# Stick-breaking attention on one core: merging the last two key blocks, holding GpSimd for scans, and re-spacing the filler matmuls

## The chip, the cores and the metric

The kernel runs on one core of one Trainium2 chip. The metric is device time in microseconds for one execution. Besides the plain time of several runs there is one profiled execution: every instruction of every engine with its start and its duration. The engines are TensorE (PE, with its weight loads as PEld), VectorE (DVE), ScalarE (ACT), GpSimd (POOL) and SyncE (SP, which only issues DMAs here).

## The reference, cut to what matters

One decoder block: RMSNorm, then a short-convolution branch and an attention branch in parallel on the same normalised input, both gated and merged, then a gated MLP. 1040 positions (16 meta tokens and 1024 real ones), width 1024, 16 heads of 64. The change lies in the attention:

```python
z = einsum(qb, kb) * scale                # one block of 128 queries, all earlier keys
log_beta = log_sigmoid(z)
log_fail = where(causal, log_beta - z, 0)
survive = cumsum(log_fail, reverse) - log_fail
a = where(causal, exp(log_beta + survive), 0)
o = einsum(a, vb)
```

So the weight of key s for query t is sigmoid(z_ts) times the product of (1 - sigmoid(z_tj)) over the keys j between s and t: a running product from the diagonal backwards.

## The kernel before, in words

**Stages.** The program has a first stage of projections (Strassen products on TensorE, up to about 670 us of the span), the attention stage (about 670 to 1028 us), a stage with the branch projections (to about 1160 us), and then the output projection and the MLP (to the end at 1966 us). Numbers are fp32 split into a high and a low fp32r part (`split`, `low`), so one product is two or three matmuls.

**The planner.** The first three stages are not written out in order. `Plan.add` collects tasks with an engine, an estimated cost, a key (a due time on the planner's own clock), dependencies, and slots that the task takes and frees (PSUM banks and buffers). `Plan.run` plays them through: whenever an engine is free it starts the ready task with the lowest key whose slots are free, and calls its `emit`, which writes the instructions. At the end `in_program_order` pins this order on each engine, so an engine that waits for one instruction also holds all behind it. The planner has a slot called `port`, one in number: GpSimd tasks and those VectorE tasks that are marked `port` (the scans at L900 among them), or that may run on either engine (`ANY`), exclude each other in planned time. On the chip nothing enforced that.

**Attention.** There are 8 pairs of heads (`p`, `h`), and the 1026 kept queries go in 9 blocks of 114 (`b`), three at a time (`g` = 0, 1, 2), which makes 48 units. In a unit each of the three query blocks gets its scores `z` on TensorE (L883, L884), ScalarE turns them into `fl` = sigmoid(-z) (L889), and VectorE runs a scan over the keys from the back (L900), 128 + 114 b elements long. Then `fl` is turned key block by key block: `turn` transposes into a PSUM bank `tp` (L919), ScalarE casts it to `ah` (L924), VectorE subtracts for the low part `al` (`low`, recorded as L353), and `weigh` multiplies both with the values into `av` (L934, L935). A unit has 3 g + 3 key blocks; to all but the last two belong three query blocks (342 columns), to the last but one two (228 columns), to the last one one (114). So the last two blocks are two steps with a bank, a cast and a subtraction each.

**A unit's end.** ScalarE copies half of `av` into the single buffer `half` (`out1`, L957), the rest into `ot` (`out2`, L960), and GpSimd adds `half` to `ot` (`out3`, L964), which frees `half`. After a pair's six units GpSimd adds the term `ends` to all 1026 columns in one operation (`last_add`, L977), and the pair is stored to DRAM.

**Fillers.** TensorE's other work in the stage are plain products (L253 to L255): two gate items and six convolution items, each 24 steps of three matmuls of 342 columns. Their weights come through ScalarE (`whi`, L367) and GpSimd (`wlo`, L275). All 24 steps of an item have keys within about 11 us of planned time; gates start at key 0 and 20, convolution items at 50 plus about 52 for each. The convolution items need the rows `y`, which take the place of the gates' input and therefore come after the last gate; `split_rows` loads, casts (L1009) and subtracts each row of 1026 columns in one operation on VectorE or GpSimd.

Of the kernel before, what the change touches and what calls it, by code (L numbers as in the profile page):

```python
# [35 lines left out]
class Plan:  # L36
    LAG = {"PE": 0.22, "ACT": 0.18, "DVE": 0.13, "POOL": 0.13, "SP": 2.5, None: 0.0}

    def __init__(self, slots, since=None):
        self.slots = dict(slots, port=1)  # L40
        self.free = dict(since.free) if since else dict.fromkeys(Plan.LAG, 0.0)
        self.tasks = []

    def add(self, engine, cost, emit, after=(), key=0.0, takes=(), frees=(),
            port=False):
        t = SimpleNamespace(engine=engine, cost=cost, emit=emit, key=key, takes=tuple(takes),
                            frees=frees, port=port or engine in ("POOL", "ANY"), users=[], left=0, number=len(self.tasks))
# [10 lines left out]
    def run(self):  # L58
        events, count, done, free = [], 0, 0, self.free
        now = free["PE"]  # L60
        ready = {e: [] for e in Plan.LAG}

        def enter(t):
            for e in ("DVE", "POOL") if t.engine == "ANY" else (t.engine,):
                insort(ready[e], (t.key, t.number, t))

        for t in self.tasks:
            if t.left == 0:
                enter(t)
        for at in free.values():  # L70
            if at > now:
                heappush(events, (at, count, True, None))
                count += 1
        while done < len(self.tasks):
            moved = True
            while moved:
                moved = False
                for e in Plan.LAG:
                    if e is not None and free[e] > now + 1e-9:
                        continue  # L80
                    for i, (_, _, t) in enumerate(ready[e]):
                        if (not t.port or self.slots["port"]) and all(
                                self.slots[k] >= t.takes.count(k) for k in t.takes):
                            break
                    else:
                        continue
                    del ready[e][i]
# [59 lines left out]
def block_kernel(ctx, tc, x, meta_tokens, g_pre_mix, w_in, channels, w_proj_conv,  # L147
# [198 lines left out]
    pin_from = len(nc.cur_bb.bb.instructions)  # L346
    plan = Plan({"raw": 2, "whi": 0, "wlo": 0, "ap": 4, "wk": 5, "st": 8, "xw": 2, "gt": 1})
# [28 lines left out]
    def plain(o, chunks, key, evac, finish, psum, first_chunk=0, given=None, w=w_in, src=src_x,  # L376
              ready=(), eng="ANY", by="ACT", lead=16.0, space=("wk",), after=()):
# [5 lines left out]
        for ci in range(first_chunk, 3):  # L383
# [7 lines left out]
            for kb in range(KB):  # L391
                at = key + (8 * (ci - first_chunk) + kb) * 3 * pe_cost(CH)
# [444 lines left out]
    FL = [2] * 6 + [1] * 3  # L837
    plan = Plan({"raw": 1, "whi": 1, "wlo": 1, "mm": 2, "z": 2, "tp": 3, "av": 1, "qk": 2, "vv": 1,
# [11 lines left out]
    DELAY = 0.6 * half_pair  # L850
    out_tiles = {}
    av_last = last_turn = None
    for p in range(NPAIR):
        ot_parts = []
        v_ld = None
        v_users = []
        for h in range(2):
# [9 lines left out]
            for g in range(3):  # L867
# [40 lines left out]
                for kb in range(nkb):  # L908
                    k0, n = KEYS[kb]
                    bs = [b for b in range(3 * g, 3 * g + 3) if P + QB * b > k0]  # L910
                    off = QB * (bs[0] - 3 * g)
                    kst = {}
                    t_k = t_av + share[g] * half_pair * kb / nkb

                    def turn(k0=k0, n=n, bs=bs, g=g, kst=kst, fls=fls):
                        tp = kst["tp"] = ps_tp.tile([P, 512], F32, name="tp", tag="tp")
                        for b in bs:
                            j = b - 3 * g
                            nc.tensor.transpose(tp[:n, QB * j:QB * (j + 1)], fls[b]["fl"][:, k0:k0 + n],  # L919
                                                ident[:QB, :QB])  # L920

                    def high(n=n, off=off, kst=kst):
                        kst["ah"] = work.tile([P, CH], F32R, name="ah", tag="ah", bufs=4)
                        nc.scalar.copy(kst["ah"][:n, off:], kst["tp"][:n, off:CH])  # L924

                    def lower(n=n, off=off, kst=kst):
# [3 lines left out]
                    def weigh(kb=kb, n=n, off=off, h=h, nkb=nkb, kst=kst, ust=ust, p=p):  # L930
                        if kb == 0:
                            ust["av"] = ps_av.tile([P, 512], F32, name="av", tag="av")[:, :CH]
                        av, w = ust["av"], v_tiles[p][:n, kb, h, :]
                        nc.tensor.matmul(av[:, off:], w, kst["ah"][:n, off:], start=(kb == 0), stop=False)  # L934
                        nc.tensor.matmul(av[:, off:], w, kst["al"][:n, off:], start=False,  # L935
                                         stop=(kb == nkb - 1))

                    m = CH - off
                    tt = plan.add("PE", 0.098 * len(bs) + 0.02, turn, (last_turn, *(scans[b] for b in bs)), t_k, ("tp",))
# [3 lines left out]
                    hh = plan.add("ACT", act_cost(m), high, (tt,), t_k, ("ah",))  # L943
                    ll = plan.add("DVE", dve_cost(m), lower, (hh,), t_k, ("al",), ("tp",))
                    last_av = plan.add("PE", 2 * pe_cost(m) + 0.08, weigh, (hh, ll, v_ld, last_av), t_k + 1,
                                       ("av",) if kb == 0 else (), ("ah", "al"))
# [24 lines left out]
                ot_parts.append(plan.add("POOL", pool_cost(CH), out3, (o1, o2), t_o, (), ("half",)))  # L971
            plan.join(z_users, ("qk",))
        plan.join(v_users, ("vv",))

        def last_add(e="POOL", p=p):
            ov = out_tiles[p][:, :NQ].rearrange("p (b n) -> p b n", n=QB)
            engine_of(e).tensor_tensor(ov, ov, ends[:, p].unsqueeze(2).to_broadcast([P, 9, QB]), op=ALU.add)  # L977
# [3 lines left out]
        plan.add("SP" if q is nc.sync else "ACT", cost, lambda p=p, q=q: q.dma_start(  # L981
            o_d[p * P:(p + 1) * P, :], out_tiles[p][:, :NQ]), (fin,), t_o + 1, (), ("ot",))
# [6 lines left out]

    nxt[0]["los"] = nxt[1]["load"] = None  # L990
    mid_last = []
    for i, (which, ob) in enumerate(mid_gates):
        evac, finish = gate_out(which, ob, work_tile, ("wk",))

        def ended(evacs, key, finish=finish):
# [3 lines left out]
        plain(48 + 8 * which + ob, CH_Q, 20.0 * i, evac, ended, bank_mm, 0, nxt[i],  # L999
              eng="POOL", lead=34.0)  # L1000

    def split_rows(kb, parts, src_d, key, after, begin=None, takes=()):
# [8 lines left out]
        def lower(e):  # L1011
            hi, lo = parts()
# [4 lines left out]
        return plan.add("ANY", any_cost(NQ), lower, (t,), key)  # L1017
# [14 lines left out]
    def conv_item(ob, key, tile_of, psum, ready, given=None):  # L1032
# [10 lines left out]
        def finish(evacs, key):  # L1043
# [5 lines left out]
              34.0, (), (ld,))  # L1049

    y_open = plan.add(None, 0.0, open_y, tuple(mid_last))
    y_ready = [split_rows(kb, lambda kb=kb: feats["y", kb], y_d, 24.0 + 2.5 * kb, (y_open,))
               for kb in range(KB)]
# [724 lines left out]
```

## Time and profile before

| | |
|---|---|
| median of 3 runs | 1968.5 us (1965.8 to 1968.56) |
| the profiled execution's own time | 1968.02 us |
| its span, first to last instruction | 1966.1 us |
| mean granted TensorE clock | 0.993 |
| TensorE matmuls | 12876 |
| scans (L900) | 144 |
| transposes (L919) | 720 |
| casts `ah` and subtractions `al` | 288 each |

A row of the grouped view reads: line, engine, operation, written tile, read tiles, shape, count, then busy us and mean ns of one, then idle time of the engine just before these instructions and what ended it. A row of the windows view reads: the stretch in us, its length, then the busy us of each engine with the number of instructions that start in it, the granted clock of TensorE as a share of full speed, the share of the DMA engines, and GB/s. A row of the timeline reads: start us, duration us, engine, line, operation, tiles, shape, count, and in brackets idle time before it. Several equal neighbours are merged into one row with a count.

### The profile page before, as it was taken

What the parts mean: (1) busy time and instruction counts of PE and PEld (TensorE: products, weight loads), DVE (VectorE), ACT (ScalarE), POOL (GpSimd) and SP (SyncE); (2) the same over time, 40 slices, a digit from 0 to 9 for tenths busy, and PEclk for the clock granted to TensorE, in tenths of its full rate; (3) what the DMA queues carried; (4) which work ended last, traced back from release to release, by engine and by line L of the source; (5) the groups of instructions that cost most, each with busy time, mean ns of one, the idle gap of its engine ahead of it and who ended that gap; (6) DMA issues with size and microseconds to landing.
All of it is one profiled execution on the core that took longest, in us unless ns stands there. A gap on an engine that the chain in (4) does not pass through costs nothing. (4 is left out here: it accounts for less than half of the span.)

```text
span 1966.1 us, 32363 instructions
## 1 busy us (share of the span) xinstructions
PE 1909.8 (97%) x12876; PEld 1793.0 (91%) x12876; DVE 1194.9 (61%) x1820; ACT 858.5 (44%) x1786; POOL 600.2 (31%) x404
## 2 busy tenths in 40 slices
PE   6999999999999999999989999899999999999997
PEld 6999999999999988999979999779889988888886
DVE  6936666665644289999973356864444454355547
ACT  5533333344444376767772224444433444321122
POOL 1110000000000023332353311256565656553453
PEclk9999999999999999999999999999999999999999
DMA  3522121455443786564427753222222121342224
GB/s 141 166 76 87 65 71 59 132 153 156 151 135 95 177 238 185 148 174 132 122 82 220 219 158 111 76 86 76 75 75 97 65 86 65 129 165 93 86 86 139
DMA packets 73842, 238.56 MB, mean 121 GB/s; under 512 B 15400, under 2 KB 17224, under 8 KB 72668
## 3 DMA queue, kind: packets, MB, share of 16 engines
q1 hardware_dynamic: 70224, 225.48, 37.3%
q10 hardware_dynamic: 3468, 11.03, 1.7%
q8 instruction: 101, 1.65, 0.4%
q14 instruction: 49, 0.40, 0.1%
HBM read 166.02 MB, written 70.46 MB: 120 GB/s over the span
## 5 line engine op out<-in xcount | busy, mean ns | idle before, releaser
L709 PE MATMUL st<-tT,s_op 128*128 128x260 f32 x864 | 245.3, 284 | 0.0
L712 PE MATMUL st<-tT,s_op 128*128 128x260 f32 x864 | 244.4, 283 | 0.0
L711 PE MATMUL st<-tT,s_op 128*128 128x260 f32 x864 | 244.3, 283 | 0.0
L184 POOL TENSOR_TENSOR a_op<-raw,a_op 128x512 fp32r<-128x512 f32 (+1 forms) x136 | 194.6, 1444 | 98.8 <-ACT a_op L183 92.2
L900 DVE TENSOR_TENSOR_SCAN fl<-fl,upper 114x128 f32<-114x128 f32 (+5 forms) x144 | 203.6, 1431 | 21.2 <-ACT fl L889 20.9
L709 PE MATMUL st<-xnT,s_op 128*128 128x260 f32 x648 | 183.1, 283 | 0.0
L712 PE MATMUL st<-xnT,s_op 128*128 128x260 f32 x648 | 182.9, 282 | 0.0
L711 PE MATMUL st<-xnT,s_op 128*128 128x260 f32 x648 | 182.3, 281 | 0.0
L1394 PE MATMUL st<-opT,a_op 128*128 128x258 f32 (+2 forms) x528 | 171.0, 324 | 3.6 <-ACT snap L1409 1.9
L353 DVE TENSOR_TENSOR s_op<-raw,s_op 128x512 fp32r<-128x512 f32 x157 | 109.9, 701 | 105.0 <-ACT s_op L665 104.5
L1396 PE MATMUL st<-opT,a_op 128*128 128x258 f32 (+2 forms) x528 | 169.3, 321 | 1.8 <-DVE opT L184 1.5
L665 ACT CAST s_op<-raw 128x512 fp32r<-128x512 f32 x162 | 100.2, 621 | 161.4 <-PE st L712 153.0
L1398 PE MATMUL st<-opT,a_op 128*128 128x258 f32 (+2 forms) x528 | 168.9, 320 | 0.0
L712 PEld LDWEIGHTS st<-tT,s_op 128*128 128x128 f32 x864 | 163.1, 189 | 0.0
L711 PEld LDWEIGHTS st<-tT,s_op 128*128 128x128 f32 x864 | 162.7, 188 | 0.0
L709 PEld LDWEIGHTS st<-tT,s_op 128*128 128x128 f32 x864 | 162.5, 188 | 0.0
L1693 DVE TENSOR_TENSOR acc<-acc,st 128x512 f32<-128x512 f32 x144 | 98.4, 686 | 90.3 <-PE st L1688 90.3
L183 ACT CAST a_op<-raw 128x512 fp32r<-128x512 f32 (+1 forms) x136 | 85.2, 634 | 155.2 <-DMA raw<-in_w_up_gate_dram 50.6
L187 DVE TENSOR_TENSOR raw<-raw 128x512 f32<-128x512 f32 x86 | 81.9, 952 | 109.7 <-POOL a_op L184 107.5
L924 ACT CAST ah<-tp 114x342 fp32r<-114x342 f32 (+3 forms) x288 | 104.5, 404 | 60.9 <-PE tp L919 58.8
L353 DVE TENSOR_TENSOR al<-tp,ah 114x342 fp32r<-114x342 f32 (+3 forms) x288 | 114.8, 439 | 24.8 <-ACT ah L924 24.1
L1396 PE MATMUL st<-opB,a_op 128*128 128x512 f32 (+2 forms) x396 | 127.6, 322 | 1.9 <-DVE opB L184 1.7
(241 smaller groups left out, 5497.5 us busy)
## 6 DMA issues: line engine op xcount, KB each, us to landing
raw<-in_w_in_dram SPq DMA_DIRECT2D x64, 512.0 KB
raw<-in_w_up_gate_dram SPq DMA_DIRECT2D x44, 512.0 KB
act_d<-owork SPq DMA_DIRECT2D x22, 512.0 KB
araw<-act_d SPq DMA_DIRECT2D x22, 512.0 KB
raw<-in_w_down_dram SPq DMA_DIRECT2D x22, 512.0 KB
qh<-qh_d SPq DMA_DIRECT2D x32, 256.5 KB
ql<-ql_d SPq DMA_DIRECT2D x32, 256.5 KB
vv_d<-vt SPq DMA_DIRECT2D x16, 512.0 KB
```

What stands on the lines that cost most here:

```text
L184: (lo_engine or nc.vector).tensor_tensor(lo, src, hi.bitcast(F32), op=ALU.subtract)
L353: eng.tensor_tensor(out, src, hi.bitcast(F32), op=ALU.subtract)
L665: nc.scalar.copy(ops[name][:, 0], src())
L709: nc.tensor.matmul(ps, wt[:, 0, c], xh, start=start and kb == 0, stop=False, skip_group_check=True)
L711: nc.tensor.matmul(ps, wt[:, 0, c], xl, start=False, stop=False, skip_group_check=True)
L712: nc.tensor.matmul(ps, wt[:, 1, c], xh, start=False, stop=kb == 3, skip_group_check=True)
L900: nc.vector.tensor_tensor_scan(fl[:, ::-1], fl[:, ::-1], upper[:, NT - nk:][:, ::-1], 1.0, op0=ALU.mult, op1=ALU.max)
L924: nc.scalar.copy(kst["ah"][:n, off:], kst["tp"][:n, off:CH])
L1394: nc.tensor.matmul(ps, wt[:, 0, k], xh, start=start and kb == 0, stop=False, skip_group_check=True)
L1396: nc.tensor.matmul(ps, wt[:, 0, k], xl, start=False, stop=False, skip_group_check=True)
L1398: nc.tensor.matmul(ps, wt[:, 1, k], xh, start=False, stop=stop and kb == 3, skip_group_check=True)
L1693: nc.vector.tensor_tensor(a, a, ps, op=ALU.add)
```

## The change

Six edits:

1. **Two key blocks in one step.** The last two key blocks of a unit share a bank: the last block's 114 columns go to the front of `tp`, the last but one's 228 behind them. One cast and one subtraction of 342 columns replace 228 and 114. The transposes and the matmuls stay the same in number and columns.
2. **Held GpSimd operations.** Where the planner starts a GpSimd task later than the task and the engine were ready (for the port, or for a buffer), the first instruction of that task now waits on a semaphore for the last port operation that was planned on VectorE. This holds for all three planned stages.
3. **Transposes in groups.** When TensorE's last task was a `turn`, the planner prefers another ready `turn` whose key is at most 2.0 behind the lowest; the planned cost of leaving a run of transposes is now 0.08 us once, instead of 0.02 per `turn` and 0.08 per `weigh`. The delay of turns behind scores goes from 0.6 to 0.7 of a head's planned time.
4. **Smaller pieces.** `last_add` runs per group of three query blocks (342 columns, three per pair) instead of once per pair, and the subtraction of `split_rows` runs in three pieces of 342 columns, each on VectorE or GpSimd.
5. **Fillers' keys spread.** A gate's steps are 2.5 times as far apart (gates at keys 0 and 30), a convolution item's 3.5 times (items at 70 plus 44 each).
6. **Buffers.** The tiles `fl0` to `fl5`, `ot` and `wk` are allocated first, so that they lie next to `upper`. Numbers and sizes of buffers stay.

The core of the diff:

```diff
 class Plan.run:
-                    for i, (_, _, t) in enumerate(ready[e]):
-                        if (not t.port or self.slots["port"]) and all(
-                                self.slots[k] >= t.takes.count(k) for k in t.takes):
+                    best = None
+                    for i, (key, _, t) in enumerate(ready[e]):
+                        if best is not None and key > best[1] + Plan.REACH:
                             break
...
+                        if best is None or t.turns:
+                            best = i, key
+                        if e != "PE" or not turning or t.turns:
+                            break
...
+                    held = e == "POOL" and t.port and now > max(t.at, free[e]) + 1e-6
+                    first = len(Plan.program())
...
+                    if held and self.last_port is not None:
+                        Plan.hold(Plan.program()[first], self.last_port)
+                    if t.port and e == "DVE":
+                        self.last_port = Plan.program()[-1]
+                    if e == "PE":
+                        t.cost += 0.08 * (turning and not t.turns)
+                        turning = t.turns
...
     FL = [2] * 6 + [1] * 3
+    for b in range(6):
+        work.tile([P, P + QB * b], F32, name="fl", tag=f"fl{b}", bufs=2)
+    for t in ("ot", "wk"):
+        work.tile([P, NT], F32, name=t, tag=t, bufs=2)
...
-    DELAY = 0.6 * half_pair
+    DELAY = 0.7 * half_pair
...
-                for kb in range(nkb):
+                lone = nkb - 2
+                for step, kbs in enumerate([(kb,) for kb in range(lone)] + [(lone, lone + 1)]):
...
+                            cols[kb, b] = QB * (b - 3 * g - (2 if kb == lone + 1 else 0))
...
-                        nc.scalar.copy(kst["ah"][:n, off:], kst["tp"][:n, off:CH])
+                        nc.scalar.copy(kst["ah"][:n], kst["tp"][:n, :CH])
...
-                        low(nc.vector, kst["al"][:n, off:], kst["tp"][:n, off:CH], kst["ah"][:n, off:])
+                        low(nc.vector, kst["al"][:n], kst["tp"][:n, :CH], kst["ah"][:n])
...
-        fin = plan.add("POOL", pool_cost(NQ), last_add, tuple(ot_parts), t_o + 1)
+                    fins.append(plan.add("POOL", pool_cost(CH), last_add, (ot_parts[g], ot_parts[-1]), t_o + 1))
...
+    G0, GS, GST = 0.0, 30.0, 2.5
+    C0, CS, CST, Y0, YS = 70.0, 44.0, 3.5, 24.0, 2.5
...
-        plain(48 + 8 * which + ob, CH_Q, 20.0 * i, evac, ended, bank_mm, 0, nxt[i],
-              eng="POOL", lead=34.0)
+        plain(48 + 8 * which + ob, CH_Q, G0 + GS * i, evac, ended, bank_mm, 0, nxt[i],
+              eng="POOL", lead=34.0, stretch=GST)
...
-        return plan.add("ANY", any_cost(NQ), lower, (t,), key)
+        return plan.join([plan.add("ANY", any_cost(CH), lambda e, c=c: lower(e, c), (t,), key)
+                          for c in range(3)])
...
-        conv_item(ob, 50.0 + (whole_time - 30.0) * ob / (KB - N_LATE), work_tile, bank_mm, y_ready)
+        conv_item(ob, C0 + CS * ob, work_tile, bank_mm, y_ready, stretch=CST)
```

More of the change, by code (lines that the diff above doesn't have):

```diff
@@ L37 @@
     LAG = {"PE": 0.22, "ACT": 0.18, "DVE": 0.13, "POOL": 0.13, "SP": 2.5, None: 0.0}
+    REACH = 2.0
+    program = hold = None
     def __init__(self, slots, since=None):
@@ L42, in __init__ @@
         self.tasks = []
+        self.last_port = None
     def add(self, engine, cost, emit, after=(), key=0.0, takes=(), frees=(),
-            port=False):
+            port=False, turns=False):
         t = SimpleNamespace(engine=engine, cost=cost, emit=emit, key=key, takes=tuple(takes),
-                            frees=frees, port=port or engine in ("POOL", "ANY"), users=[], left=0, number=len(self.tasks))
+                            frees=frees, port=port or engine in ("POOL", "ANY"), turns=turns, users=[], left=0, number=len(self.tasks))
         for d in after:
@@ L80, in run @@
                         continue
-                    for i, (_, _, t) in enumerate(ready[e]):
-                        if (not t.port or self.slots["port"]) and all(
-                                self.slots[k] >= t.takes.count(k) for k in t.takes):
+                    best = None
+                    for i, (key, _, t) in enumerate(ready[e]):
+                        if best is not None and key > best[1] + Plan.REACH:
                             break
-                    else:
+                        if (t.port and not self.slots["port"]) or any(
+                                self.slots[k] < t.takes.count(k) for k in t.takes):
+                            continue
+                        if best is None or t.turns:
+                            best = i, key
+                        if e != "PE" or not turning or t.turns:
+                            break
+                    if best is None:
                         continue
+                    i = best[0]
+                    t = ready[e][i][2]
                     del ready[e][i]
@@ L346, in block_kernel @@
     pin_from = len(nc.cur_bb.bb.instructions)
+    Plan.program = staticmethod(lambda: nc.cur_bb.bb.instructions)
+    Plan.hold = staticmethod(lambda ins, before: tc.add_manual_dep(
+        ins, before.name, mybir.DependencyInfo(mybir.DependencyClass.Sync, mybir.DependencyReason.DATA),
+        reason="port"))
     plan = Plan({"raw": 2, "whi": 0, "wlo": 0, "ap": 4, "wk": 5, "st": 8, "xw": 2, "gt": 1})
@@ L376, in plain @@
     def plain(o, chunks, key, evac, finish, psum, first_chunk=0, given=None, w=w_in, src=src_x,
-              ready=(), eng="ANY", by="ACT", lead=16.0, space=("wk",), after=()):
+              ready=(), eng="ANY", by="ACT", lead=16.0, space=("wk",), after=(), stretch=1.0):
         st = raw_weights(o, w, key - lead) if given is None else given
@@ L391, in plain @@
             for kb in range(KB):
-                at = key + (8 * (ci - first_chunk) + kb) * 3 * pe_cost(CH)
+                at = key + (8 * (ci - first_chunk) + kb) * 3 * stretch * pe_cost(CH)
                 before = plan.add("PE", 3 * pe_cost(n), lambda kb=kb, step=step: step(kb),
@@ L912, in block_kernel, with turn @@
                     kst = {}
-                    t_k = t_av + share[g] * half_pair * kb / nkb
-                    def turn(k0=k0, n=n, bs=bs, g=g, kst=kst, fls=fls):
+                    t_k = t_av + share[g] * half_pair * step / (nkb - 1)
+                    def turn(n=n, cols=cols, kst=kst, fls=fls):
                         tp = kst["tp"] = ps_tp.tile([P, 512], F32, name="tp", tag="tp")
-                        for b in bs:
-                            j = b - 3 * g
-                            nc.tensor.transpose(tp[:n, QB * j:QB * (j + 1)], fls[b]["fl"][:, k0:k0 + n],
+                        for (kb, b), at in cols.items():
+                            k0 = KEYS[kb][0]
+                            nc.tensor.transpose(tp[:n, at:at + QB], fls[b]["fl"][:, k0:k0 + n],
@@ L932, in weigh @@
                             ust["av"] = ps_av.tile([P, 512], F32, name="av", tag="av")[:, :CH]
[L933 to L939, printed above, removed]
+                        for kb in kbs:
+                            off = QB * max(0, kb - 3 * g)
+                            at = 0 if kb == nkb - 1 else off
+                            av, w = ust["av"][:, off:], v_tiles[p][:n, kb, h, :]
+                            for k, a in enumerate(("ah", "al")):
+                                nc.tensor.matmul(av, w, kst[a][:n, at:at + CH - off],
+                                                 start=(kb == 0 and k == 0),
+                                                 stop=(kb == nkb - 1 and k == 1))
@@ L940, in block_kernel @@
+                    spent = sum(2 * pe_cost(CH - QB * max(0, kb - 3 * g)) for kb in kbs)
+                    tt = plan.add("PE", 0.098 * len(cols), turn, (last_turn, *(scans[b] for b in bs)), t_k,
+                                  ("tp",), turns=True)
                     last_turn = tt
@@ L942, in block_kernel @@
                         readers[b].append(tt)
[L943 to L946, printed above, removed]
+                    hh = plan.add("ACT", act_cost(CH), high, (tt,), t_k, ("ah",))
+                    ll = plan.add("DVE", dve_cost(CH), lower, (hh,), t_k, ("al",), ("tp",))
+                    last_av = plan.add("PE", spent, weigh, (hh, ll, v_ld, last_av), t_k + 1,
+                                       ("av",) if kbs[0] == 0 else (), ("ah", "al"))
                 for b in scans:
@@ L1009, in high, with lower @@
             nc.scalar.copy(parts()[0], parts()[1].bitcast(F32))
[L1011 to L1012 removed]
+        def lower(e, c):
+            hi, lo = (v[:, CH * c:CH * (c + 1)] for v in parts())
             low(engine_of(e), lo, lo.bitcast(F32), hi)
@@ L1030, in open_y, with conv_item @@
             feats["y", kb] = t[:, 0, kb, :NQ], t[:, 1, kb, :NQ]
-    def conv_item(ob, key, tile_of, psum, ready, given=None):
+    def conv_item(ob, key, tile_of, psum, ready, given=None, stretch=1.0):
         u = {}
```

35 lines of the change are left out of this document (20 added, 15 removed).

## The prediction

> **What bounds the kernel now.** I read the page first, then the windows view over the stretch that the diff touches, then the same view for the tile `mm` alone (the fillers), and last the groups by form and the timeline where something stood out.
>
> ```profile
> span 1966.1 us, 32363 instructions
> PE 1909.8 (97%) x12876; PEld 1793.0 (91%) x12876; DVE 1194.9 (61%) x1820; ACT 858.5 (44%) x1786; POOL 600.2 (31%) x404
> ```
> ```profile
> core 0: us, PE busy (x) PEld busy (x) DVE busy (x) ACT busy (x) POOL busy (x), PEclk, DMA share, GB/s
> 100.00:650.00 550.00, 550.00 (x4569) 550.00 (x4568) 318.09 (x496) 226.42 (x459) 34.60 (x26) 1.00 0.35 110
> 1030.00:1150.00 120.00, 120.00 (x763) 120.00 (x762) 42.10 (x74) 25.40 (x40) 36.09 (x30) 1.00 0.76 223
> ```
> ```profile
> 670.00:700.00 30.00, 29.80 (x201) 29.17 (x200) 17.84 (x22) 15.44 (x38) 3.82 (x3) 1.00 1.02 251
> 720.00:980.00 260.00, 254.34 (x1773) 237.43 (x1772) 246.51 (x353) 187.09 (x488) 83.11 (x54) 1.00 0.58 161
> 980.00:1003.50 23.50, 20.64 (x140) 17.57 (x138) 21.19 (x34) 19.42 (x50) 13.54 (x7) 1.00 0.32 104
> 1003.50:1010.50 7.00, 6.85 (x30) 6.01 (x28) 3.83 (x7) 3.44 (x10) 4.38 (x3) 0.51 0.10 35
> 1010.50:1028.50 18.00, 15.50 (x107) 13.16 (x106) 14.65 (x25) 14.09 (x35) 9.30 (x5) 1.00 0.09 31
> ```
> ```profile
> 670.00:1028.50 358.50, 346.11 (x2369) 321.01 (x2368) 318.26 (x457) 253.51 (x650) 119.71 (x76) 0.99 0.58 158
> ```
>
> The page's averages (TensorE 97%, VectorE 61%) hide two regimes. Before 650 us and from 1030 to 1150 us TensorE is busy without a gap: the change adds no work there and can win none. In attention (670 to 1028.5 us) TensorE is idle 12.4 of 358.5 us, and VectorE is busy 318.3. From 720 to 980 us VectorE has 246.5 of 260 us, 95%, and TensorE 254.3, 98%: both are nearly full, and neither alone sets the pace. At the end, from 980 us, TensorE loses 5.5 us outright, and for 7 us its clock is halved.
>
> ```profile
> 670.00:714.00 44.00, 26.46 (x144) 22.83 (x144) 0.00 (x0) 3.28 (x6) 1.00 0.89 219
> 714.00:740.00 26.00, 5.13 (x19) 3.10 (x19) 0.00 (x0) 0.00 (x0) 1.00 0.87 245
> 740.00:980.00 240.00, 81.10 (x410) 65.69 (x410) 7.86 (x16) 0.00 (x0) 1.00 0.56 155
> 980.00:1028.50 48.50, 0.77 (x4) 0.60 (x5) 0.92 (x2) 0.00 (x0) 0.93 0.20 67
> ```
>
> These are the fillers. All 144 gate matmuls are gone by 714 us, the next 26 us get 19, and the last 48.5 us get 4. Where they are missing, TensorE can only do what attention has ready.
>
> **The change part by part.** All against the profiled execution, 1968.0 us (span 1966.1 and 1.9 around it), which lies 0.5 below the median shown.
>
> *Two key blocks in one step.*
>
> ```profile
> L353 DVE TENSOR_TENSOR al<-tp,ah 114x342 fp32r<-114x342 f32 x144 | 67.6, 499 | 16.6 <-ACT ah L924 16.2
> L353 DVE TENSOR_TENSOR al<-tp,ah 114x228 fp32r<-114x228 f32 x48 | 18.3, 382 | 0.7 <-ACT ah L924 0.5 <-PE av L934 0.3
> L353 DVE TENSOR_TENSOR al<-tp,ah 114x114 fp32r<-114x114 f32 x48 | 12.5, 259 | 0.8 <-ACT ah L924 0.7
> ```
> ```profile
> 788.61 1.33 DVE L353 TENSOR_TENSOR al<-tp,ah 114x342 fp32r<-114x342 f32 x3
> 789.85 4.24 DVE L900 TENSOR_TENSOR_SCAN fl<-fl,upper 114x1040 f32<-114x1040 f32 x1
> ```
>
> By durations a unit saves 382 + 259 - 499 = 142 ns of VectorE, 6.8 us for 48. But neighbours overlap: three of 499 ns took 1.33 us, so each hides (1.497 - 1.33) / 2 = 0.08 us of the next. One operation fewer hides one overlap fewer: 0.06 us each, 3.0 us. I take -3, with 6.8 as the far end. ScalarE drops 48 casts as well; at 253.5 of 358.5 us it isn't the bound, so I count nothing. Transposes and matmuls stay.
>
> *GpSimd operations held for the scan.*
>
> ```profile
> 787.16 2.25 POOL L964 TENSOR_TENSOR ot<-ot,half 64x342 f32<-64x342 f32 x1 [0.49 <-ACT ot L960]
> 789.38 2.54 POOL L275 TENSOR_TENSOR wlo<-raw,whi 128x512 fp32r<-128x512 f32 x2
> ```
> ```profile
> L900 DVE TENSOR_TENSOR_SCAN fl<-fl,upper 114x1040 f32<-114x1040 f32 x16 | 40.4, 2524 | 2.3 <-ACT fl L889 2.3
> L900 DVE TENSOR_TENSOR_SCAN fl<-fl,upper 114x926 f32<-114x926 f32 x16 | 33.5, 2095 | 0.0
> L900 DVE TENSOR_TENSOR_SCAN fl<-fl,upper 114x698 f32<-114x698 f32 x16 | 28.1, 1756 | 1.9 <-ACT fl L889 1.9
> L900 DVE TENSOR_TENSOR_SCAN fl<-fl,upper 114x584 f32<-114x584 f32 x16 | 23.1, 1447 | 1.8 <-ACT fl L889 1.6
> L900 DVE TENSOR_TENSOR_SCAN fl<-fl,upper 114x356 f32<-114x356 f32 x16 | 14.3, 892 | 1.2 <-ACT fl L889 1.2
> L900 DVE TENSOR_TENSOR_SCAN fl<-fl,upper 114x128 f32<-114x128 f32 x16 | 7.7, 484 | 9.6 <-ACT fl L889 9.6
> ```
>
> The scan at 789.85 takes 4.24 us against a mean of 2.52 for its size, and ends 2.2 us after the two `wlo` pieces ended (791.92): it ran behind them, not beside them. How much is lost that way? A line through the 926 and 356 rows has 2.11 ns per element; by it 1040, 698, 584 and 128 should take 2336, 1614, 1373 and 411 ns. They take 188, 142, 74 and 73 more; times 16 that is 7.6 us of scans that stood behind GpSimd. Holding removes only those where the planner had put the GpSimd task second, and not those planned ahead of a late scan. So between 0 and -7.6; I take -4, half.
>
> The Trainium skill ("SBUF — State Buffer", "Who interferes with whom") says that a VectorE instruction with two SBUF inputs and a GpSimd instruction that reads SBUF exclude each other for the whole instruction, and that the one issued first decides who blocks. The trace agrees: 2.25 us for a `half` addition that meets a scan, 4.24 for a scan that meets two `wlo`. The rule speaks against this edit where the scan is first anyway, which is a rival below.
>
> What a hold costs: GpSimd is in order, so behind a held `out3` queue `wlo` pieces (a filler on TensorE needs them) and the next `out3`; who waits for `out3` is `out1`, for the single buffer `half`. GpSimd is busy 119.7 of 358.5 us, which covers that; without the cover it is the slower rival. In the first stage the same hold sits under a TensorE that is full for 550 of 550 us, with 26 GpSimd operations in all: nothing; if a held operand came late, TensorE would show gaps there.
>
> *Smaller pieces.*
>
> ```profile
> L964 POOL TENSOR_TENSOR ot<-ot,half 64x342 f32<-64x342 f32 x47 | 61.8, 1316 | 205.4 <-ACT ot L960 198.3 <-DVE fl L900 6.8
> L977 POOL TENSOR_TENSOR ot<-ot,ends 128x1026 f32<-128x1026 f32 x7 | 16.9, 2412 | 0.6
> L353 DVE TENSOR_TENSOR yT<-yT 128x1026 fp32r<-128x1026 f32 x7 | 8.3, 1205 | 0.0
> ```
>
> Sixteen GpSimd operations more in `last_add`: 24 at up to 1.3 us instead of 8 of 2.4, at most +12 us on an engine with 239 us idle: hidden. Their gain is that none blocks a scan for 2.4 us. Of eight `y` subtractions seven ran on VectorE, 8.3 us, at the fullest time. In thirds some fit on GpSimd between scans. If all go, -8.3; if none goes, 14 operations more at 0.06 us, +0.8. I take -3, a third of the way.
>
> *Grouped transposes, later turns.* No row prices a switch alone. The stretch 720 to 980 us has one matmul per 147 ns; 48 steps fewer can save at most one such spacing each, -7, but all matmuls stay, so I take -0.5, near zero; if the grouping keeps a score or an `av` waiting, a few tenths come back (+1).
>
> *Fillers spread.* The hole 714 to 740 us and the end get fillers that now crowd the middle. Gain: 7 us at half clock cost 3.4, and the tail's idle is 5.5.
>
> ```profile
> 996.03 3.56 POOL L977 TENSOR_TENSOR ot<-ot,ends 128x1026 f32<-128x1026 f32 x1
> 999.56 2.92 POOL L964 TENSOR_TENSOR ot<-ot,half 64x342 f32<-64x342 f32 x1
> 1002.24 0.43 PE L935 MATMUL av<-al,vv 114*128 114x342 f32 x1 [1.59 <-DVE al L353]
> ```
>
> This is how the slow clock came about: `last_add` and `out3` around a scan, `al` late behind it, TensorE without a filler, and from 1003.5 us the clock at 0.51. The Trainium skill ("TensorE: Matmul & The Clock Gate", "Part 1: The HAM clock gate") asks for an idle window of about 3.4 us before the clock halves; the longest wait here is 1.59. The measurement decides; by the rule alone nothing was to be regained and the sum would be 3.4 smaller. I take the clock, -3.4, and -3 of the 5.5, since `al` there is late for VectorE's sake too; far end -8.9, near end 0.
>
> *Buffers.* Cover: TensorE busy 29.8 of 30 us from 670, and 120 of 120 from 1030. If a new tile waited longer for its old reader than fillers last, it would show as a gap there; 0, and a gain has nothing to take.
>
> The sum: VectorE terms 3 + 4 + 3 = 10, of which I pass on 0.6, because TensorE is at 98% beside it: 6. Fillers 6.4, transposes 0.5. Together 12.9, less about 1 for waits that appear anew: -12. So 1968.0 - 12 = 1956.
>
> **The rivals.**
>
> *More than that.* All far ends on VectorE, 6.8 + 7.6 + 8.3 = 22.7, less a third that TensorE can't follow, plus 8.9: -24, 1944. For it: VectorE at 95%. Against it: TensorE at 98% in the same window.
>
> *Nothing.* The chip's own exclusion already makes a late GpSimd operation wait, the freed VectorE time lands under a full TensorE, and the fillers only change places; the halved clock returns elsewhere: 0 to -3, about 1967. For it: `half` additions that waited without a semaphore, 2.25 and 2.92 us long. The Trainium skill's rule on the shared port ("Who interferes with whom", above) gives the same wherever the scan comes first. Against it: the 7.6 us of scans that did stand behind.
>
> *Slower: the hold closes on `half`.*
>
> ```profile
> ACT half L957 <- PE av L935: 16.2, 25, 1.7
> ```
>
> ScalarE's waits for `half` are all put down to TensorE today, none to GpSimd. A held `out3` behind a held pair of `wlo` frees `half` after a scan (2.52), one `wlo` (1.27) and itself (1.32): 5.1 us. The shortest unit, 0.18 of a head's 358.5 / 16 = 22.4 us, lasts 4.0. Then `out1` stands 1.1 us, and behind it on ScalarE the casts and sigmoids, thus scans and transposes. At 16 short units that is 17.6 us; with 12 gained, +5.6, about 1974, and up to 1986 without the gains. It decides from the point where `out3`'s wait exceeds 4.0 us. Against it: GpSimd idle two thirds of the stage.
>
> **How the numbers follow.** About 0.2% of this kernel, 4 us, is what a measurement can tell from no change. Chances: forecast 0.52 (own range 1949 to 1963), more 0.15, nothing 0.18, slower 0.15. The range from 1945 to 1973 leaves out about half of "more" and most of "slower", together 0.2. Faster: 0.52 + 0.15 + 0.03 from "nothing" with its small gains = 0.70; same 0.15; slower 0.15.
>
> **What would show it.** Right: attention ends some 12 us earlier; subtractions `al` number 240; scans of 1040 stay near 2.3 us; more than 4 filler matmuls in the last 48 us and no clock at 0.5 there. Wrong: scans as long as before (the hold hits nothing), ScalarE waiting for `half` on GpSimd (the slower rival), VectorE's busy time down by 10 but the stage as long (TensorE sets the pace), or gaps of TensorE after 1030 us or before 650 (buffers, holds).

## The result and the profile after

The changed kernel takes 1954.8 us in the median of 4 runs (1953.33 to 1957.61) against 1968.53 before: a ratio of 0.9931, with a 95% interval of 0.9912 to 0.995. Run once more beside other kernels it gave 0.9934 (0.992 to 0.9947). That is 13 to 14 us faster; 1956 was forecast. But the profile does not show the sum that the forecast was made of.

The page of the changed kernel, and its windows view (columns as before: length, then busy us of PE, PEld, DVE, ACT and POOL, clock, DMA share, GB/s):

```profile
span 1951.5 us, 32323 instructions
PE 1901.7 (97%) x12876; PEld 1790.2 (92%) x12876; DVE 1194.6 (61%) x1798; ACT 854.3 (44%) x1738; POOL 570.5 (29%) x426
```
```profile
100.00:650.00 550.00, 550.00 (x4568) 550.00 (x4567) 317.00 (x496) 226.30 (x459) 27.37 (x26) 1.00 0.37 110
1020.00:1135.00 115.00, 115.00 (x730) 114.94 (x729) 40.15 (x77) 23.70 (x38) 31.82 (x28) 1.00 0.77 224
```
```profile
670.00:1013.50 343.50, 336.79 (x2371) 318.41 (x2370) 322.73 (x429) 249.68 (x602) 101.28 (x98) 1.00 0.64 165
```
```profile
670.00:700.00 30.00, 30.00 (x209) 29.45 (x208) 23.73 (x27) 18.53 (x45) 4.28 (x4) 1.00 1.04 223
720.00:980.00 260.00, 257.59 (x1831) 243.76 (x1829) 253.61 (x341) 193.04 (x470) 77.11 (x74) 1.00 0.61 165
980.00:1006.50 26.50, 22.21 (x154) 19.48 (x154) 25.10 (x35) 20.18 (x46) 12.56 (x13) 1.00 0.32 97
1006.50:1010.50 4.00, 4.00 (x21) 3.64 (x19) 2.33 (x6) 2.45 (x6) 2.97 (x4) 0.57 0.02 4
```

Attention ends at 1013.5 instead of 1028.5 us: the whole gain is there, since before and after it TensorE is full as it was. In this stage VectorE does not work less. It is busy 322.7 us instead of 318.3; its idle time went from 40.2 to 20.8. The first 30 us show 23.7 us of VectorE instead of 17.8. TensorE was idle 12.4 us and is now idle 6.7, and for the same number of matmuls it is busy 336.8 us instead of 346.1. Of these 9.3 us the halved clock explains about 1.7 (7.0 us at 0.51 before, 4.0 at 0.57 now); no run here takes the rest apart.

What VectorE waited for, in the waits view of its engine over the attention stage (total us, times, longest), first of the kernel before, then of the changed one:

```profile
DVE al L353 <- ACT ah L924: 24.1, 30, 1.8
DVE fl L900 <- ACT fl L889: 20.9, 13, 9.6
```
```profile
DVE fl L931 <- ACT fl L920: 15.5, 12, 9.5
DVE al L380 <- ACT ah L959: 9.0, 18, 1.1
```

The wait of subtractions for their cast went down by 15.1 us, the scans' wait for sigmoids by 5.4. That is an account of where the 15 us show on VectorE (19.4 us less idle time, 4.5 us more work); which edit brought them, only the experiments can tell.

The groups by form, in the same stage of the changed kernel:

```profile
L380 DVE TENSOR_TENSOR al<-tp,ah 114x342 fp32r<-114x342 f32 x192 | 89.3, 495 | 8.1 <-ACT ah L959 8.1
L380 DVE TENSOR_TENSOR yT<-yT 128x342 fp32r<-128x342 f32 x22 | 11.3, 565 | 0.8 <-ACT yT L1053 0.8
L380 POOL TENSOR_TENSOR yT<-yT 128x342 fp32r<-128x342 f32 x2 | 2.1, 1050 | 0.0
L1015 POOL TENSOR_TENSOR ot<-ot,ends 128x342 f32<-128x342 f32 x23 | 27.1, 1177 | 1.8
L1004 POOL TENSOR_TENSOR ot<-ot,half 64x342 f32<-64x342 f32 x48 | 42.1, 877 | 203.4 <-DVE fl L931 81.2 <-ACT ah L959 45.4 <-ACT ot L1000 28.2
```
```profile
L931 DVE TENSOR_TENSOR_SCAN fl<-fl,upper 114x1040 f32<-114x1040 f32 x16 | 39.5, 2469 | 1.5 <-ACT fl L920 1.5
L931 DVE TENSOR_TENSOR_SCAN fl<-fl,upper 114x926 f32<-114x926 f32 x16 | 34.8, 2174 | 0.8 <-ACT fl L920 0.8
L931 DVE TENSOR_TENSOR_SCAN fl<-fl,upper 114x698 f32<-114x698 f32 x16 | 28.0, 1750 | 0.2 <-ACT fl L920 0.2
L931 DVE TENSOR_TENSOR_SCAN fl<-fl,upper 114x584 f32<-114x584 f32 x16 | 24.5, 1531 | 1.6 <-ACT fl L920 1.6
L931 DVE TENSOR_TENSOR_SCAN fl<-fl,upper 114x356 f32<-114x356 f32 x16 | 15.0, 939 | 0.0
L931 DVE TENSOR_TENSOR_SCAN fl<-fl,upper 114x128 f32<-114x128 f32 x16 | 7.9, 494 | 9.5 <-ACT fl L920 9.5
```

The holds are there: `out3` (now L1004) waited 81.2 us for scans (`fl` L931), and its own mean fell from 1316 to 877 ns, since most of its waiting now comes ahead of its record and not inside it. But the scans did not get shorter: 1040 and 698 elements lost 55 and 6 ns, 926, 584, 356 and 128 gained 79, 84, 47 and 10. By the page's line all 144 are busy 206.6 us, and were 203.6. And of 24 pieces of `y` GpSimd took two; VectorE spends 11.3 us on them instead of 8.3.

The fillers, in the windows of the tile `mm`:

```profile
670.00:714.00 44.00, 22.68 (x114) 18.27 (x114) 0.00 (x0) 2.19 (x4) 1.00 1.03 222
714.00:740.00 26.00, 7.94 (x38) 5.91 (x36) 0.00 (x0) 1.10 (x2) 1.00 0.80 250
980.00:1013.50 33.50, 3.39 (x17) 2.73 (x18) 0.50 (x1) 0.00 (x0) 0.95 0.25 77
```

The hole at 714 us has 38 filler matmuls instead of 19, the last 33.5 us have 17, where the last 48.5 had 4.

### The profile page after: what moved, and what is told of

Its sections match the earlier page's. It is cut to its first block, busy times and chain, and to the rows that moved or that the text cites. A ratio compares the mean times of both kernels' runs of the same rounds, so it can differ in the third digit from the quotient of the medians.

```text
span 1951.5 us, 32323 instructions
## 1 busy us (share of the span) xinstructions
PE 1901.7 (97%) x12876; PEld 1790.2 (92%) x12876; DVE 1194.6 (61%) x1798; ACT 854.3 (44%) x1738; POOL 570.5 (29%) x426
## 5 line engine op out<-in xcount | busy, mean ns | idle before, releaser
L931 DVE TENSOR_TENSOR_SCAN fl<-fl,upper 114x470 f32<-114x470 f32 (+5 forms) x144 | 206.6, 1458 | 15.6 <-ACT fl L920 15.5
L1441 PE MATMUL st<-opB,a_op 128*128 128x512 f32 (+2 forms) x396 | 127.8, 323 | 0.9 <-DVE opB L207 0.8
L1439 PE MATMUL st<-opB,a_op 128*128 128x512 f32 (+2 forms) x396 | 127.8, 323 | 0.0
L1443 PE MATMUL st<-opB,a_op 128*128 128x512 f32 (+2 forms) x396 | 127.4, 322 | 0.0
```

What stands on the lines that cost most here:

```text
L931: nc.vector.tensor_tensor_scan(fl[:, ::-1], fl[:, ::-1], upper[:, NT - nk:][:, ::-1], 1.0, op0=ALU.mult, op1=ALU.max)
L1439: nc.tensor.matmul(ps, wt[:, 0, k], xh, start=start and kb == 0, stop=False, skip_group_check=True)
L1441: nc.tensor.matmul(ps, wt[:, 0, k], xl, start=False, stop=False, skip_group_check=True)
L1443: nc.tensor.matmul(ps, wt[:, 1, k], xh, start=False, stop=stop and kb == 3, skip_group_check=True)
```

## The experiments

Two theories stood against each other after this profile. The **prediction's**: each edit takes work or waits off VectorE, and 0.6 of that reaches the end. The **order theory**: VectorE's work is hardly changed, and what was won is that TensorE's fixed order hands ScalarE and VectorE their next step in time. All ratios are to the kernel before, run beside each kernel, with their 95% intervals. Against the changed kernel's 0.9934, 0.001 is 2 us.

**The changed kernel again**, for scatter.

> The changed kernel once more, beside the kernels below on one chip. Every theory: 0.993 of the kernel before. It gives the scatter from chip to chip, against which the one before has to be read.

Measured: 1953.68 us, 0.9934 (0.992 to 0.9947). Its scans start within 0.2 us of those of the first profile throughout attention: the order repeats so well that two traces can be laid over each other. One thing does not repeat, the slow clock near the end of attention:

```profile
1006.00:1012.50 6.50, 6.25 (x44) 5.01 (x43) 4.49 (x10) 3.92 (x10) 3.53 (x4) 1.00 0.01 3
```

The same matmul waits 1.90 us for its `al` shortly before (1.89 in the first profile), and here the clock stays at 1.00.

**Without the hold**, twice:

```diff
-                    held = e == "POOL" and t.port and now > max(t.at, free[e]) + 1e-6
+                    held = False
```

> The changed kernel without the hold: GpSimd tasks start as soon as their data is there. The prediction's theory (a hold removes half of the scans' wait behind GpSimd): 4 us slower than the changed kernel, about 1959, and scans over 144 sum to some 210 us instead of 206.6. The rival theory (the hold releases GpSimd just as a scan ends, and it then stands ahead of the next scan, so nothing is won): 1952 to 1956, scans at 207 us or less.

> The changed kernel without the hold, once more: the plan and with it the order on every engine are the changed kernel's, only the semaphore waits are gone. If the hold is worth the 3.5 us that the first comparison gave, 0.9948 against 0.993 beside it. If that was scatter, the two lie within 0.001. In both cases the scans' sum is lower without the hold, by about 3 us, as it was the first time: it is not the scans through which a hold can win.

Measured: 1957.09 us, 0.9949 (0.9937 to 0.9962), and 1956.95 us, 0.9948 (0.9936 to 0.996). So about 3 us are lost without the hold, the same both times; the intervals still overlap that of the changed kernel. By ratio that is nearer to the prediction's 4 us than to the rival's nothing; the scans are as the rival had them. First the scans' line of the page and the attention stage of the changed kernel run beside it, then the same of the kernel without the hold:

```profile
L931 DVE TENSOR_TENSOR_SCAN fl<-fl,upper 114x470 f32<-114x470 f32 (+5 forms) x144 | 206.5, 1457 | 15.5 <-ACT fl L920 15.4
```
```profile
670.00:1012.50 342.50, 335.58 (x2370) 316.92 (x2369) 322.64 (x429) 249.86 (x602) 101.33 (x98) 1.00 0.63 165
```
```profile
L931 DVE TENSOR_TENSOR_SCAN fl<-fl,upper 114x470 f32<-114x470 f32 (+5 forms) x144 | 203.1, 1435 | 16.5 <-ACT fl L920 16.5
```
```profile
670.00:1017.00 347.00, 337.08 (x2375) 317.76 (x2374) 320.96 (x429) 250.21 (x603) 116.19 (x98) 1.00 0.62 164
```

Without the hold the scans take 3.4 us less, and the stage is 4.5 us longer: VectorE idles 26.0 us instead of 19.9. One place in the timelines (start us, us) shows it; without the hold, VectorE and GpSimd:

```profile
907.59 4.27 DVE L931 TENSOR_TENSOR_SCAN fl<-fl,upper 114x242 f32<-114x242 f32 x3
```
```profile
908.74 0.87 POOL L1004 TENSOR_TENSOR ot<-ot,half 64x342 f32<-64x342 f32 x1 [1.02 <-ACT ot L1000]
909.58 1.28 POOL L298 TENSOR_TENSOR wlo<-raw,whi 128x512 fp32r<-128x512 f32 x1
```

and with it:

```profile
905.46 2.47 DVE L931 TENSOR_TENSOR_SCAN fl<-fl,upper 114x242 f32<-114x242 f32 x3
```
```profile
908.08 0.79 POOL L1004 TENSOR_TENSOR ot<-ot,half 64x342 f32<-64x342 f32 x1 [2.49 <-DVE fl L931]
```

The same three scans (of 242, 356 and 470 elements; a merged row shows the first one's shape) take 4.27 us where two GpSimd operations come in between, and 2.47 where the first of these is held until the scans are through. The whole difference lies in the third: its record is 2.91 us long without the hold and 1.11 with it. Half of that is paid a moment later: with the hold the next scan, of 584 elements, stands behind the `wlo` piece and takes 2.24 us instead of 1.36. So the hold does not remove the exclusion; it moves it to another scan. The Trainium skill ("SBUF — State Buffer", "Who interferes with whom") has issue order, and not an operation's shape, decide who blocks; these rows agree.

**GpSimd's additions cut to two columns.** This kernel leaves out most of the sums at a unit's and a pair's end.

```diff
-                    engine_of(e).tensor_tensor(o, o, ust["half"][a0:a0 + 64], op=ALU.add)
+                    engine_of(e).tensor_tensor(o[:, :2], o[:, :2], ust["half"][a0:a0 + 64, :2], op=ALU.add)
```

> The changed kernel with the GpSimd additions at a unit's and a pair's end cut to two columns (the rest of the sums is left out); plan, order and waits stay. It takes away the GpSimd time that scans stand behind, but for weights and rows. The prediction's theory (VectorE's waits pass on by 0.6): the scans lose about 6 us of their 210, the kernel is 4 us faster than the changed one. The rival (a scan that waits is caught up by TensorE's slack or the order elsewhere): within 1 us.

Measured: 1950.79 us, 0.9919 (0.9907 to 0.9932). The scans' line of its page, and its attention stage:

```profile
L931 DVE TENSOR_TENSOR_SCAN fl<-fl,upper 114x470 f32<-114x470 f32 (+5 forms) x144 | 197.1, 1392 | 17.7 <-ACT fl L920 17.6
```
```profile
670.00:1011.50 341.50, 334.74 (x2369) 316.91 (x2369) 314.48 (x429) 250.15 (x603) 46.76 (x98) 1.00 0.62 166
```

The scans lose 9.4 us, and the last product of attention ends 1.4 us earlier (1011.3 against 1012.7); VectorE's idle time is 27.0 instead of 19.9. By medians the whole is 3 us faster, with intervals that overlap. So 0.1 to 0.3 of the work taken off VectorE reached the end, not 0.6: VectorE waited the longer elsewhere.

**Old keys for all fillers, and for the gates alone.**

```diff
-    G0, GS, GST = 0.0, 30.0, 2.5
+    G0, GS, GST = 0.0, 20.0, 1.0
...
-        conv_item(ob, C0 + CS * ob, work_tile, bank_mm, y_ready, stretch=CST)
+        conv_item(ob, 50.0 + (whole_time - 30.0) * ob / (KB - N_LATE), work_tile, bank_mm, y_ready)
```

For the gates alone only the first pair of lines is changed.

> The changed kernel with the fillers' keys of before (gates at 0 and 20, convolution items at 50 plus 51.6 each, steps not stretched). The prediction's theory (the fillers win 6.4 us, mostly at the end of attention): about 1961, with no filler in the last 40 us of attention. The rival theory (nearly all of the 13.7 us is VectorE's idle time that the order of the fillers removes, at the start of attention above all): 1964 to 1968, and VectorE idle again by some 12 us in the first 50 us of attention.

> The changed kernel with the two gates' keys of before (0 and 20, not stretched), the convolution items spread. The rival theory that the start of attention is where the fillers' order pays (VectorE busy 40 us in the first 50 us instead of 34): 6 to 8 us slower than the changed kernel, nearly all that the undone spread cost. The prediction's theory (the end of attention is where it pays): within 2 us.

Measured: 1961.54 us, 0.9973 (0.9963 to 0.9983) with all keys old; 1961.18 us, 0.9976 (0.9966 to 0.9985) with the gates' alone. Both lose 8 us. The first 30 us of attention, of the kernel with all keys old and of that with the gates' alone:

```profile
670.00:700.00 30.00, 29.94 (x201) 29.11 (x200) 18.57 (x21) 15.13 (x35) 3.51 (x3) 1.00 1.03 256
```
```profile
670.00:700.00 30.00, 29.43 (x194) 28.67 (x193) 16.57 (x18) 14.44 (x33) 3.51 (x3) 1.00 1.03 245
```

VectorE does 18.6 and 16.6 us of work there, the changed kernel 23.7. TensorE is busy 29.4 us or more in each; with the old keys it runs 109 and 102 filler matmuls and 38 and 36 for scores there, in the changed kernel 79 and 46. What the spread wins, it wins at the start: with all keys old the 37th `av` matmul of the stage, at 708 us in the changed kernel, comes 6.8 us later, and the last one 7.5 later. (The profiled execution of the second kernel is 5 us above its median, so no more than its start is read.)

**The spread alone, on the kernel before; then with the new layout of buffers.** The diff is the change's edit 5 alone, and then with edit 6.

> The kernel before with only the fillers' keys spread (gates at 0 and 30 at 2.5 times the distance, convolution items at 70 plus 44 each at 3.5 times). The prediction's theory: 6.4 us faster than before, by the end of attention. The rival that the order is most of the gain: 8 to 10 us faster, VectorE busy some 40 us instead of 32 in the first 50 us of attention. If the spread needs the other edits to pay: 0 to 4 us.

> The kernel before with the fillers spread and the buffers laid out anew. If the layout is what made the spread alone 10 us slower than before: 0 to 8 us faster than before. If the spread needs the merged blocks and the grouped transposes to pay (the order theory): still 6 us or more slower than before, though without the wait for a store.

Measured: 1976.84 us, 1.0053 (1.0041 to 1.0066), and 1976.46 us, 1.0051 (1.0037 to 1.0065): both 10 us slower than before. All three forecasts for the first had it faster; for the second the order theory's "6 us or more slower" held. Two stretches of the first:

```profile
740.00:760.00 20.00, 17.18 (x95) 15.66 (x94) 15.63 (x20) 14.55 (x33) 6.12 (x5) 0.83 1.01 292
1000.00:1041.00 41.00, 31.19 (x188) 27.93 (x188) 31.41 (x45) 26.28 (x64) 13.56 (x9) 0.83 0.21 65
```

TensorE's waits for `al` come to 10.3 us in either kernel's attention (4.7 before), and in parts of these two stretches the clock halves. (The profiled execution of the first is 4 us above its median; that of the second is its median, and shows 13.7 us at half clock in attention, the kernel before 6.8.) The edit that is worth 8 us in the full change costs 10 in the kernel before. The layout isn't the reason, since the second kernel is as slow. Nor does the spread fail at the start: there the 37th `av` matmul of the second kernel comes 10.6 us earlier than in the kernel before. It loses that, and more, later in the stage.

**The old layout of buffers**: the five lines of edit 6 left out.

> The changed kernel with the attention's buffers laid out as before. The prediction's theory (nothing waits for an old reader longer than fillers last): within 1 us of the changed kernel. The rival, from one wait of 2.4 us for a store in the kernel before with spread fillers (a sigmoid that waits for the DMA whose tile lay where its own now lies): 3 to 8 us slower than the changed kernel, with a wait of ScalarE for a store in the first 50 us of attention.

Measured: 1955.23 us, 0.9945 (0.9932 to 0.9957), about 2 us lost, within the intervals. One row of ScalarE's waits and the first 30 us:

```profile
ACT fl L916 <- DMA ga_d<-su: 1.8, 1, 1.8
```
```profile
670.00:700.00 30.00, 28.58 (x197) 27.60 (x195) 20.20 (x23) 16.92 (x41) 4.27 (x4) 1.00 1.03 233
```

A sigmoid waits 1.8 us for the store of a gate's tile, and VectorE has 20.2 us of work at the start instead of 23.7. From the 37th `av` matmul until 978 us the changed kernel is 2.4 to 2.5 us ahead. The rival mechanism is there; its price is below the 3 us that it was given.

**The last two blocks in two steps again**: the loop over `(kb,)` for all key blocks, with its 228 and 114 columns.

> The changed kernel with the last two key blocks in two steps again: 288 casts and subtractions. The prediction's theory (3 us of VectorE, 0.6 of it passed on): 1957. The rival theory (two short steps at each unit's end are two links of a chain through TensorE, ScalarE and VectorE, so more than the work is lost): 1960 or more.

Measured: 1958.89 us, 0.9964 (0.9951 to 0.9978), 6 us lost. Its attention stage:

```profile
670.00:1018.50 348.50, 336.95 (x2369) 319.23 (x2368) 327.69 (x478) 255.98 (x651) 96.68 (x97) 1.00 0.61 162
```

The time lies between the prediction's 1957 and the rival's 1960. VectorE is busy 5.0 us more than in the changed kernel, the stage is 5.0 us longer, and the idle time is the same, 20.8. But not all of that work is the edit's. The tile `al` alone, in the changed kernel and in this one:

```profile
670.00:1013.50 343.50, 84.80 (x288) 55.17 (x288) 109.48 (x240) 1.00 0.64 165
670.00:1018.50 348.50, 86.06 (x288) 55.04 (x288) 113.32 (x288) 1.00 0.61 162
```

The subtractions take 3.8 us of VectorE more; most of the rest are row subtractions for keys and values: three of `kk` and two of `vv` at a mean of 0.69 and 1.02 us, where the changed kernel has one and two of about 0.5. So the totals match, but that work is passed on in full is not shown: the two links of the chain per unit that the rival names would look the same.

**No grouping of transposes, old switch costs and delay:**

```diff
-                                  ("tp",), turns=True)
+                                  ("tp",))
...
-    DELAY = 0.7 * half_pair
+    DELAY = 0.6 * half_pair
```

> The changed kernel without grouped transposes, with the planned switch costs of before and the delay of 0.6. The prediction's theory (0.5 us): 1955 to 1956. The rival theory (TensorE's order, not the work, is what was won, and a run of transposes cuts switches that the page hides in busy time): 1959 to 1962, with more runs of transposes than the 142 of the changed kernel.

Measured: 1958.08 us, 0.9954 (0.9942 to 0.9967), 4 us lost, between the prediction's 1955 to 1956 and the rival's 1959 to 1962, with 188 runs of transposes counted in the trace against 142 (the kernel before has 167). The planned costs of before, 0.02 per `turn` and 0.08 per `weigh`, are back in this kernel too; whether the costs, the grouping or the delay matter was not tried apart. Until 919 us the kernel is at most 1.0 us behind at the places of the table below, and its attention has 6.8 us at half clock near the end, which cost up to 3.4.

**Whole pieces again**: `last_add` once per pair, a row's subtraction in one operation.

> The changed kernel with a pair's last addition and a row's subtraction in one operation each again. The prediction's theory (3 us of VectorE, 0.6 passed on): 2 us slower than the changed kernel. Against it stands that the profile after has 22 of 24 pieces of y on VectorE, 11.3 us instead of 8.3; by that alone it would be 0 to 2 us faster. A rival: GpSimd operations of 2.4 us that scans stand behind, as the planner's port foresees them, cost the order: 4 us slower or more.

Measured: 1960.84 us, 0.997 (0.9958 to 0.9981), 7 us lost. Its attention stage, one row of VectorE's waits, and the rows of `y`:

```profile
670.00:1020.50 350.50, 340.45 (x2367) 322.23 (x2366) 315.62 (x409) 251.88 (x603) 92.12 (x76) 0.98 0.60 161
```
```profile
DVE al L380 <- ACT ah L959: 23.1, 30, 2.3
```
```profile
L380 DVE TENSOR_TENSOR yT<-yT 128x1026 fp32r<-128x1026 f32 x5 | 7.8, 1565 | 1.7 <-ACT yT L1051 1.7
L380 POOL TENSOR_TENSOR yT<-yT 128x1026 fp32r<-128x1026 f32 x3 | 7.1, 2393 | 0.0
```

With whole pieces VectorE works 7.1 us less and the stage is 7 us longer: the subtractions wait 23.1 us for their casts, about as long as in the kernel before. Part of the 7 us is TensorE's clock, which was halved three times in this stage:

```profile
759.00:764.00 5.00, 5.00 (x28) 5.00 (x27) 5.00 (x7) 2.04 (x5) 1.55 (x2) 0.66 1.02 237
998.00:1006.00 8.00, 6.25 (x28) 5.82 (x29) 6.50 (x8) 3.89 (x7) 2.38 (x1) 0.57 0.00 0
1012.00:1016.00 4.00, 4.00 (x24) 3.95 (x23) 2.52 (x5) 2.58 (x7) 0.44 (x1) 0.57 0.00 0
```

These rows lose up to 6.9 us to the clock (length times one minus the clock); the same sum is 1.7 in the first profile of the changed kernel and 0 in the second. Over its six executions the mean clock was 0.991 to 0.993, over the nine of the changed kernel 0.992 to 0.996. Even without the clock's share the 7.1 us of work taken off VectorE brought nothing, which decides against counting VectorE's work. That the later subtractions made the clock fall is likely but not shown, since the same wait in the changed kernel came with and without a fall.

**Where each loss arises.** The traces of all kernels have the 576 `av` matmuls of attention in the same order. The table says, for one profiled execution each, how many us later than in the second run of the changed kernel the same one starts (in the head, its time there), and how long the clock was halved in the stage. A minus sign means earlier.

| | 37th, 708 us | 145th, 780 | 253rd, 839 | 397th, 919 | 576th, 1012 | us at half clock |
|---|---|---|---|---|---|---|
| without the hold | 1.3 | 1.5 | 1.3 | 3.6 | 4.3 | 0 |
| all keys old | 6.8 | 5.1 | 8.3 | 7.9 | 7.5 | 0 |
| last two blocks in two steps | -1.5 | -0.3 | 4.0 | 4.2 | 5.5 | 3.4 |
| no grouping | 0.0 | 0.6 | -1.5 | 1.0 | 5.7 | 6.8 |
| whole pieces | -0.3 | 1.5 | 3.8 | 3.4 | 7.6 | 13.7 |
| kernel before | 8.6 | 4.6 | 10.7 | 17.5 | 15.9 | 6.8 |
| before, spread, new layout | -2.0 | 3.2 | 7.0 | 14.5 | 21.8 | 13.7 |

The fillers' loss is there after 40 us and stays. The hold's comes in good part between 839 and 919 us, where the place shown above lies. The grouping's comes after 919 us.

## Why the prediction was right in its total and wrong in its sum

The time and the stage were right: 1956 against 1954.8, all of it in attention, with nothing from the stages around it. That the total came out is luck: VectorE's part of the sum had the wrong sign for its work, and other terms were too small. The step that failed is "VectorE terms 3 + 4 + 3 = 10, of which I pass on 0.6", in the terms as in the factor. VectorE's busy time did not fall by 10 us but rose by 4.5, and 19.4 us of its idle time went. Point by point:

- *Two blocks in one step, -3.* The work was sized well: 3.8 us of `al`. In time, undoing it costs about 6 us instead of the 1.8 that 0.6 of 3 would be.
- *The hold, -4 through shorter scans.* Worth about 3, but not through the scans: they sum to 3.4 us less without it. The count of 7.6 us was of the right size: against each size's median before, all nine sizes together are 10.1 us too long. That the hold would remove half of it was wrong: the same count is 14.0 us in the changed kernel and 10.7 without the hold. In the rows shown a held operation starts as a scan ends, and the one behind it meets the next scan.
- *Smaller pieces, -3 by moving work to GpSimd.* Wrong sign for the work: two pieces of 24 moved, VectorE got 3.0 us more of `y`, and with whole pieces the scans are shorter (202.2 us by the page's line). Undoing it still costs 7 us, with longer waits for casts and a slower clock.
- *Grouping, -0.5.* Undoing edit 3 costs 4, late in the stage, and in the profiled execution partly by the clock.
- *Fillers, -6.4, by the end of attention.* The size fits, 8; the place doesn't: it is the start. The end still has TensorE idle for 4.3 us from 980 to 1006.5. The stretch at half clock there (7.0 us at 0.51 before) is 4.0 us at 0.57 in the first profile and missing in the second, so the -3.4 for the clock is not told apart from scatter.
- *Buffers, 0.* About 2, at the start, where cover was claimed because TensorE was full. TensorE was; the wait lay on ScalarE.

Of the rivals, the slower one did not come: `out1` waited for TensorE alone. "Nothing" was right that the exclusion stays, and wrong that the fillers would only change places. TensorE's clock halved in the changed kernel with no wait of TensorE over 1.9 us in the stage, as before with 1.6; so the idle window of about 3.4 us that the Trainium skill names ("TensorE: Matmul & The Clock Gate", "Part 1: The HAM clock gate") was not needed here either. Nor is such a wait enough: with 1.90 us in the second profile the clock did not fall.

What stays open: undone one at a time, the hold costs 3 us, the fillers' keys 8, the grouping 4, the merged blocks 6, the buffers 2 and the pieces 7, 30 together, and all of them won 13; the spread alone costs 10. So they are no sum. Every one but the hold and the buffers makes the planner write another order, and the keys may simply fit this set of edits. Whether a small shift of one key in the changed kernel costs as much was not measured, so of the 4 to 8 us of each undone edit it isn't told apart how much is the edit, how much a less fitting order, and how much the clock that such an order meets. The clearest of them is the fillers' 8 us: they arise at the start, with no slow clock, and the spread gains at least as much at the start of the kernel before.

## What to carry to other kernels

With two engines at 95% and 98% and a fixed order, count idle time by what ended it, and not busy time alone: here 15 us less of waits of one subtraction for its cast went with the gain, and 8 and 7 us of work taken off VectorE brought little and nothing. A semaphore that makes the chip keep the planned order can win, here about 3 us, though it shortens nothing; that a wait is cheaper where the plan foresees it is the likely reason, seen at one place only. Spread fillers so that the first steps of the long chain go ahead of them, and measure edits of an order together: alone, one of these cost 10 us. Lay two traces over each other at the same matmuls before saying where a loss arises, and look at the clock of each.

## What the runs showed of the hardware that was not expected

A scan that meets GpSimd operations waits them out whole: a scan of 470 elements took 2.91 us or 1.11, by whether two GpSimd operations of 2.15 us together came in between, and ended 1.0 us after the second. The other way round a `half` addition waits for the scan: a mean of 1316 ns before, 877 where a semaphore took most of the waiting out of its record. The subtraction of `y` in thirds has a mean of 565 ns against 495 for `al` of as many columns. Nearly all of that comes from four of the 22 pieces, 564 to 1225 ns long, and these four are the ones whose record overlaps one of GpSimd; the other 18 take 479 to 516. Both inputs of `y` lie in SBUF; one input of `al` lies in PSUM. Of the 288 `al` records in the kernel before, 133 overlap one of GpSimd by 0.1 us or more, and none is longer than 516 ns.

TensorE's clock can fall or not fall after the same wait in the same order: 1.89 us in one execution with 3.4 us at half clock behind it, 1.90 us in another with none.
